# Delta rule: the inverse of the triangular systems kept as 64 columns per row

## The chip, the cores and the metric

The kernel runs on one core of a Trainium2 chip. The metric is the device time of one execution in microseconds, from launch to the last output. Three runs of the kernel before took 1076.86, 1078.5 and 1078.3 us; the median is 1078.3 us. The profiled execution is a further one, with its own time.

A core has a matrix engine (TensorE, PE in the rows), a vector engine (VectorE, DVE), a scalar engine (ScalarE, ACT), GpSimd (POOL) and SyncE (SP), which issues the transfers. Each works off its own queue in order and waits on semaphores for the others. TensorE takes its operands from the on-chip memory SBUF and writes to PSUM, eight banks of 128 partitions by 512 floats. Every matmul has a weight load ahead of it (rows named PEld), which can overlap the matmul before. A plain float32 product of this kernel is recorded as two loads and two matmuls, a product of rounded float32 halves and a transpose as one of each.

## The reference, cut to what matters

One layer of a hybrid encoder for 512 prompt rows and 64 sample rows: a gated delta rule (4 heads of 128) beside a differential attention, then attention to a memory, then a feed-forward block, with norms between. The change is in the delta rule. For each head it works on chunks of rows and solves two triangular systems:

```python
a_sys = jnp.where(strict, bc[..., :, None] * kk * gam, 0.0) + jnp.eye(C)
u = lax.linalg.triangular_solve(a_sys, bc[..., None] * vc, lower=True, unit_diagonal=True)
w = lax.linalg.triangular_solve(a_sys, (bc * jnp.exp(G))[..., None] * kc, lower=True, unit_diagonal=True)
```

after which a scan over the chunks carries the state: `vn = u - w S`, the output `qg S + qk vn`, and the new `S`.

## The kernel before, in words

The 576 rows (512 and 64) are worked through in five delta-rule chunks: four of 128 rows and the last of 64. The reference's chunk is 64 rows; a chunk of 128 is the same recurrence with a larger system. The order of the whole kernel: input norm and its transposes, projections of k, q and v with a short convolution, the gates, the norm of the memory rows, then `gdn_prep` and `gdn_scan` for the chunks, with the projection of z (`project_z`) and, later in the program, the projections and heads of the attention. After that come the output projection, the attention to the memory and the feed-forward block, all of them long rows of projections (`project`).

`gdn_prep` prepares one chunk: transposes of k, q and v, the decay matrix `gam`, the system `At` (transposed, strictly upper triangular, four heads side by side), and then its inverse by doubling (lines 595 to 643). The inverse is held twice: `X`, upper triangular, and `Dt`, its transpose. `masked(lv)` picks out of `At` the entries that couple two blocks of lv rows; `lev` holds the level of each entry. At the start `X` is the identity minus level 1, and `Dt` its transpose. Each level lv = 2, 4, 8, 16, 32 then does, for the four heads:

1. `by` = product of the masked `B` (weights) and `Dt` (moving), copied to `Y` by ScalarE (line 619);
2. `bx` = product of `X` (weights) and `Y` (moving), subtracted from `Dt` by VectorE (line 624);
3. four transposes of `Dt`, copied to `X` by ScalarE (line 628).

Level 64, the last doubling, only fills the block of `X` above the diagonal (lines 634 to 642). Until then both 64-row halves of a 128-row system are separate: `X` and `Dt` are block diagonal with two blocks of 64 by 64, and the other two quarters of each are zeros, which are multiplied and copied along. In the last chunk, of 64 rows, there is one block, and the level 32 is its last.

The products of a chunk go to one PSUM bank, `g0` for even chunks and `g1` for odd ones, each with one buffer. So a chunk's next product waits until the bank's last one is read. Two chunks' preparations run beside each other, one in each bank. The scans use the bank `gs`; the projections use `pr`, three buffers.

What sets the order: the framework's planner draws it at build time, from the order of the program, the dependencies and its own durations for the instructions; an instruction that is ready in that plan goes ahead of a later one. Around the change no order is written out by hand (that is only so in the opening, `in_order`). Semaphores are then placed for that fixed order on each engine. All matmuls carry line 99 and all transposes line 105, those of the helpers `mm` and `tr`.

Of the kernel before, what the change touches and what calls it, by code (L numbers as in the profile page):

```python
# [11 lines left out]
ALU = mybir.AluOpType  # L12
# [3 lines left out]
P = 128  # L16
# [8 lines left out]
H = 4  # L25
# [9 lines left out]
def hybrid_layer_kernel(  # L35
# [10 lines left out]
    V, A, G = nc.vector, nc.scalar, nc.gpsimd  # L46
# [28 lines left out]
    def nm(s):  # L75
        uid[0] += 1
        return f"{s}_{uid[0]}"
# [6 lines left out]
    def small(tag, shape, bufs=None):  # L84
        tag = SHARED.get(tag, tag)
        bufs = 1 if tag in ("vn", "on", "S") or tag[:-1] in ("At", "Dt", "Y") else 2
        return sp.tile(shape, F32, tag=tag, name=nm(tag), bufs=bufs)
# [4 lines left out]
    def bank(tag="ba"):  # L92
        return ps.tile([P, 512], F32, tag=tag, name=nm(tag), bufs=BANKS[tag])
# [4 lines left out]
    def mm(out, lhsT, rhs, start=True, stop=True, pin=False):  # L98
        i = nc.tensor.matmul(out, lhsT, rhs, start=start, stop=stop)  # L99
        if pin:  # L100
            tc.keep_in_program_order(i)

    def tr(out, in_, pin=False):
        n = in_.shape[0]
        i = nc.tensor.transpose(out, in_, ident[:n, :n])  # L105
        if pin:
            tc.keep_in_program_order(i)

    def bc(col, shape):
        return col.to_broadcast(shape)  # L110
# [110 lines left out]
    def turn(src, n, q, tag):  # L221

        b = bank(tag)
        for i in range(4):
            tr(b[:, i * P : i * P + n], src[:n, (4 * q + i) * P : (4 * q + i + 1) * P])
        return b.rearrange("p (i t) -> p i t", i=4)[:, :, :n]
# [138 lines left out]
    for typ in (1, 0, 2):  # L365
        cT[typ] = unit({1: 4, 0: 5, 2: 6}[typ], [P, 4, T])
        for h in range(H):
# [7 lines left out]
            n = SOFF + DEC  # L375
# [106 lines left out]
    for bi in range(2):  # L482
        scale(mn[:, bi, :], mt[:, bi, :], root(squares(mn[:, bi, :], mt[:, bi, :], P), P), gkv, P)
        for q in range(2):
            src = turn(mn[:, bi, :], P, q, "ba")
# [5 lines left out]
    with tc.issue_after(opened[mybir.EngineType.DVE]), tc.issue_after(opened[mybir.EngineType.Pool]):  # L491
        lev = const([P, P], "lev")
        prev = ident
        for lb in range(7):
            s = 2 << lb
            e = small("X", [P, P])
            G.memset(e, 1.0)
# [16 lines left out]
    def v4(ap, n):  # L514
        return ap.rearrange("p (h n) -> p h n", h=4)[:, :, :n]

    def sb(tag, bufs=2):
        return small(tag, [P, 4, P], bufs)
# [10 lines left out]
    def gdn_prep(c, c0, n):  # L529
        L = slice(c0, c0 + n)  # L530

        def st(tag):
            return sb(dict(gam="Y", sq="B", eg="B").get(tag, tag) + str(c % 2))

        r8 = tiny([P, 8], "tg")
        s8 = tiny([P, 8], "tg")
        bk = bank(f"g{c % 2}")
        for h in range(H):
            tr(bk[:n, h * P : (h + 1) * P], ck[:, h, L])
        kd = sb("kd")  # L540
        V.tensor_tensor(kd[:n], v4(bk, P)[:n], kdc[:n, c, :].unsqueeze(2).to_broadcast([n, 4, P]), ALU.mult)
        sq = st("sq")
        A.activation(sq[:n], v4(bk, P)[:n], AF.Square)
        V.tensor_reduce(s8[:n, 0:4], sq[:n], AX.X, ALU.add)
        bq = bank(f"g{c % 2}")
        for h in range(H):
            tr(bq[:n, h * P : (h + 1) * P], cq[:, h, L])
        sq2 = st("sq")
        A.activation(sq2[:n], v4(bq, P)[:n], AF.Square)
        V.tensor_reduce(s8[:n, 4:8], sq2[:n], AX.X, ALU.add)  # L550
        V.tensor_scalar(s8[:n], s8[:n], EPS, None, ALU.add)
        rpow(r8[:n], s8[:n])
        brk = tiny([P, 4], "tg")
        V.reciprocal(brk[:n], s8[:n, 0:4])
        V.tensor_tensor(brk[:n], brk[:n], beta[:n, c, :], ALU.mult)

        bg = bank(f"g{c % 2}")
        for h in range(H):
            mm(bg[:, h * P : h * P + n], bc(gg[:n, c, h : h + 1], [n, P]), triu[:n, :n])
        gam = st("gam")  # L560
        for h in range(H):
            V.tensor_scalar(
                gam[:n, h, :n], bg[:n, h * P : h * P + n], Gc[:n, c, h : h + 1], 0.0, ALU.subtract, ALU.min
            )
        A.activation(gam[:n, :, :n], gam[:n, :, :n], AF.Exp)
        G.tensor_tensor(gam[:n, :, :n], gam[:n, :, :n], triu[:n, :n].unsqueeze(1).to_broadcast([n, 4, n]), ALU.mult)
        bkk = bank(f"g{c % 2}")
        for h in range(H):
            mm(bkk[:n, h * P : h * P + n], ck[:, h, L], ck[:, h, L])
        At = st("At")  # L570
        for h in range(H):
            V.scalar_tensor_tensor(
                At[:n, h, :n], bkk[:n, h * P : h * P + n], brk[:n, h : h + 1], gam[:n, h, :n], ALU.mult, ALU.mult
            )
        bkq = bank(f"g{c % 2}")
        for h in range(H):
            mm(bkq[:n, h * P : h * P + n], ck[:, h, L], cq[:, h, L])
        KQ = sb("KQ")
        V.tensor_tensor(KQ[:n, :, :n], v4(bkq, n)[:n], gam[:n, :, :n], ALU.mult)
        nk, rq2 = tiny([P, 4], "tg"), tiny([P, 4], "tg")  # L580
        V.tensor_tensor(nk[:n], s8[:n, 0:4], r8[:n, 0:4], ALU.mult)
        V.tensor_scalar(r8[:n, 4:8], r8[:n, 4:8], P ** -0.5, None, ALU.mult)
        V.tensor_tensor(rq2[:n], r8[:n, 4:8], r8[:n, 4:8], ALU.mult)
        bv = bank(f"g{c % 2}")
        for h in range(H):
            tr(bv[:n, h * P : (h + 1) * P], cv_[:, h, L])
        vb = sb("vb")
        V.tensor_tensor(vb[:n], v4(bv, P)[:n], nk[:n].unsqueeze(2).to_broadcast([n, 4, P]), ALU.mult)
        if c > 0:
            eg = st("eg")  # L590
            A.activation(eg[:, :, :n], v4(bg, n), AF.Exp)
            G.tensor_tensor(ck[:, :, L], ck[:, :, L], eg[:, :, :n], ALU.mult)
            G.tensor_tensor(cq[:, :, L], cq[:, :, L], eg[:, :, :n], ALU.mult)  # L593

        def masked(lv):
            B = st("B")
            V.scalar_tensor_tensor(  # L597
                B[:n, :, :n], lev[:n, :n].unsqueeze(1).to_broadcast([n, 4, n]), float(lv), At[:n, :, :n],
                ALU.is_equal, ALU.mult,
            )  # L600
            return B

        X = sb("X")
        Dt = st("Dt")
        B = masked(1)
        V.tensor_tensor(X[:n, :, :n], ident[:n, :n].unsqueeze(1).to_broadcast([n, 4, n]), B[:n, :, :n], ALU.subtract)
        bt = bank(f"g{c % 2}")
        for h in range(H):
            tr(bt[:n, h * P : h * P + n], X[:n, h, :n])
        A.copy(Dt[:n, :, :n], v4(bt, n)[:n])  # L610
        lv = 2
        while lv < n:
            Y = st("Y")
            by = bank(f"g{c % 2}")
            if lv < 64:
                B = masked(lv)
                for h in range(H):
                    mm(by[:n, h * P : h * P + n], B[:n, h, :n], Dt[:n, h, :n])
                A.copy(Y[:n, :, :n], v4(by, n)[:n])
                bx = bank(f"g{c % 2}")  # L620
                if 2 * lv < n:
                    for h in range(H):
                        mm(bx[:n, h * P : h * P + n], X[:n, h, :n], Y[:n, h, :n])
                    V.tensor_tensor(Dt[:n, :, :n], Dt[:n, :, :n], v4(bx, n)[:n], ALU.subtract)  # L624
                    bt = bank(f"g{c % 2}")
                    for h in range(H):
                        tr(bt[:n, h * P : h * P + n], Dt[:n, h, :n])
                    A.copy(X[:n, :, :n], v4(bt, n)[:n])  # L628
                else:
                    for h in range(H):  # L630
                        mm(bx[:n, h * P : h * P + n], Y[:n, h, :n], X[:n, h, :n])
                    V.tensor_tensor(X[:n, :, :n], X[:n, :, :n], v4(bx, n)[:n], ALU.subtract)
            else:
                for h in range(H):
                    mm(by[64:, h * 64 : h * 64 + 64], At[:64, h, 64:], Dt[:64, h, :64])
                A.copy(Y[64:, :, :64], by[64:, :256].rearrange("p (h n) -> p h n", h=4))
                bx = bank(f"g{c % 2}")
                for h in range(H):
                    mm(bx[:64, h * 64 : h * 64 + 64], Y[64:, h, :64], X[64:, h, 64:])
                V.tensor_scalar(  # L640
                    X[:64, :, 64:], bx[:64, :256].rearrange("p (h n) -> p h n", h=4), -1.0, None, ALU.mult
                )
            lv *= 2
        return dict(kd=kd, vb=vb, X=X, KQ=KQ, brk=brk, rq=r8[:, 4:8], rq2=rq2)
# [291 lines left out]
    cols, rB = norm_columns(), const([P, T], "rB")  # L936
# [16 lines left out]
    for h in range(H):  # L953
# [8 lines left out]
        for t, (q0, _) in enumerate(QT):  # L962
            t0, n = TT[t]
# [7 lines left out]
            p = small("p0", [P, 512])  # L971
# [3 lines left out]
            bt = bank()  # L975
# [23 lines left out]
    cols, rB = norm_columns(), const([P, T], "rB")  # L999
# [90 lines left out]
    for m in range(KT):  # L1090
        last_block(m, pend, *HALVES[1])
        if m == 1:
            r = final_roots((0, 1), pin=True)
# [7 lines left out]
    r = final_roots((2, 3, 4))  # L1101
# [37 lines left out]
```

## Time and profile before

| | |
|---|---|
| median of three runs | 1078.3 us |
| profiled execution | 1076.9 us, its span from first to last instruction 1075.2 us |
| mean granted TensorE clock | 0.996 |
| matmul and weight-load instructions | 7504 each |
| weight reads and other reads from memory | 79.14 MB, 83 GB/s over the span with the writes |
| doubling products and transposes | first at 143.1 us, last at 284.8 us after the span's start |

A row of groups has the line, the engine, the operation, the tiles written and read, the shape, the count, then busy time in us and the mean duration of one in ns, then the engine's idle time just before them with what ended it. For TensorE the shape is weights (rows*columns), then the moving side. Matmuls overlap each other, so their durations are longer than the distance between them. A row of waits has the engine and tile, the instruction that released it, the total in us, the number of waits and the longest. A row of the timeline has the start in us, the length in us, the engine, the line, and a count where instructions of one kind follow each other.

### The profile page before, as it was taken

The page shows a single profiled execution, that of the slowest core. Times are in us where ns is not written, and L with a number is a line of the kernel's source. Part 1 is how long each engine was busy: PE and PEld are TensorE (multiplying, and loading weights), DVE is VectorE, ACT ScalarE, POOL GpSimd, SP SyncE. Part 2 cuts the span into 40 slices and gives each one's busy share as a digit, 9 for nine tenths or more (in the row PEclk, how much of TensorE's full clock was granted, in tenths as well). Part 3 has the DMA queues.
Part 4 walks back from the last instruction along what each step waited for, and adds up shares of the span by engine and source line. Part 5 has one row for each costly group of instructions (what it writes and reads, how often), then busy time and mean ns, then how long its engine had stood idle before and what let it go on. Part 6 is the DMA issues. An engine that isn't in the chain of part 4 may idle for free.

```text
span 1075.2 us, 18514 instructions
## 1 busy us (share of the span) xinstructions
PE 1043.5 (97%) x7504; PEld 982.4 (91%) x7504; DVE 625.2 (58%) x1347; ACT 401.3 (37%) x824; POOL 69.9 (6%) x126
## 2 busy tenths in 40 slices
PE   6999989899999999999999999999999999999996
PEld 5999989888888877999888899999999999999996
DVE  6756783666466765564554555555555555555654
ACT  5433644333246566443333443222222222222344
POOL 3311120222000000000000000000000000000000
PEclk9999999999999999999999999999999999999999
DMA  7242410010132265625111122132324141313312
GB/s 208 66 148 60 133 36 21 25 37 21 40 100 62 62 189 158 194 80 157 40 52 48 40 81 77 50 102 65 100 59 118 50 118 49 110 51 114 91 50 89
DMA packets 139448, 90.06 MB, mean 84 GB/s; under 512 B 5522, under 2 KB 130576, under 8 KB 138852
## 3 DMA queue, kind: packets, MB, share of 16 engines
q1 hardware_dynamic: 139364, 88.89, 28.3%
q8 instruction: 59, 0.97, 0.4%
q14 instruction: 25, 0.20, 0.1%
HBM read 79.14 MB, written 9.74 MB: 83 GB/s over the span
## 4 chain that ended last, share of the span: by engine, by line
PE 87%; issue 5%; DVE 3%; POOL 2%; DMA 1%; SPq 1%; ACT 1%; POOLq 0%; DVEq 0%; ACTq 0%
PE pr L99 69%; PE g L99 8%; PE gs L99 3%; PE ba L105 3%; PE ba L99 2%; PE g L105 2%; DMA raw<-in_w_in_dram 1%; POOL tg L185 1%; DVE B L597 1%; SPq L120 0%; POOL tiny L185 0%; DVE wl L153 0%; DVE u L213 0%; DVE Dt L624 0%; POOL u L593 0%
## 5 line engine op out<-in xcount | busy, mean ns | idle before, releaser
L99 PE MATMUL pr<-u,wh 128*128 128x256 f32 (+1 forms) x3552 | 733.1, 300 | 0.4 <-DVE u L269 0.3
L99 PEld LDWEIGHTS pr<-u,wh 128*128 128x128 f32 x3552 | 575.3, 190 | 5.8 <-issue 2.4
L99 PE MATMUL pr<-u,wl 128*128 128x256 f32 (+1 forms) x1776 | 529.3, 299 | 0.0
L99 PEld LDWEIGHTS pr<-u,wl 128*128 128x128 f32 x1776 | 336.0, 190 | 2.0 <-issue 0.7
L152 ACT CAST wh<-raw 128x1024 fp32r<-128x1024 f32 (+1 forms) x153 | 136.5, 892 | 269.6 <-PE pr L99 249.6
L153 DVE TENSOR_TENSOR wl<-raw,wh 128x1024 fp32r<-128x1024 f32 (+1 forms) x153 | 157.4, 1029 | 60.2 <-ACT wh L152 57.9
L901 DVE TENSOR_TENSOR u<-u,pr 128x256 f32<-128x256 f32 (+1 forms) x160 | 72.2, 453 | 102.1 <-PE pr L99 101.4
L1010 DVE TENSOR_TENSOR p<-pr,rB 128x256 f32<-128x256 f32 x64 | 29.3, 458 | 63.2 <-PE pr L99 63.2
L178 ACT CAST u<-p 128x256 fp32r<-128x256 f32 x64 | 27.8, 434 | 88.7 <-DVE p L1011 86.9
L185 POOL TENSOR_TENSOR tiny<-tiny,nhalf 128x1 f32<-128x1 f32 (+4 forms) x11 | 8.5, 773 | 670.1 <-DVE tiny L1069 413.3
L99 PE MATMUL pr<-wh,u 128*128 128x512 f32 x128 | 42.0, 404 | 0.0
L179 DVE TENSOR_TENSOR u<-p,u 128x256 fp32r<-128x256 f32 x64 | 29.3, 457 | 20.2 <-ACT u L178 20.2
L99 PE MATMUL pr<-u,u 128*128 128x256 f32 (+1 forms) x240 | 34.9, 305 | 0.0
L99 PEld LDWEIGHTS pr<-u,u 128*128 128x128 f32 x240 | 33.4, 197 | 0.0
L1011 DVE SCALAR_TENSOR_TENSOR p<-p 128x256 f32<-128x256 f32 x64 | 29.3, 458 | 1.7
L99 PE MATMUL g<-u,qz 128*128 128x256 f32 (+4 forms) x96 | 29.6, 411 | 0.3 <-ACT p L810 0.3
L628 ACT COPY X<-g 128x512 f32<-128x512 f32 (+1 forms) x24 | 13.2, 550 | 41.0 <-PE g L105 38.1
L379 DVE SCALAR_TENSOR_TENSOR p<-p,gcol,p 128x579 f32<-128x579 f32 x33 | 27.1, 822 | 1.1
L99 PEld LDWEIGHTS pr<-wh,u 128*128 128x128 f32 x128 | 23.4, 188 | 4.5 <-issue 0.2
L181 ACT ACTIVATE u<-u,gcol 128x256 fp32r<-128x256 f32 (+1 forms) x32 | 17.1, 534 | 23.5 <-DVE u L901 23.5
L99 PE MATMUL g<-Dt,B 128*128 128x128 f32 (+1 forms) x200 | 25.6, 272 | 0.1
L99 PE MATMUL pr<-wl,u 128*128 128x512 f32 x64 | 25.6, 400 | 0.0
(284 smaller groups left out, 1075.8 us busy)
## 6 DMA issues: line engine op xcount, KB each, us to landing
raw<-in_w_ff_dram SPq DMA_DIRECT2D x32, 512.0 KB
raw<-in_w_ff_dram SPq DMA_DIRECT2D x64, 256.0 KB
raw<-in_w_in_dram SPq DMA_DIRECT2D x28, 512.0 KB
raw<-in_w_mem_k_dram SPq DMA_DIRECT2D x8, 512.0 KB
raw<-in_w_mem_v_dram SPq DMA_DIRECT2D x8, 512.0 KB
raw<-in_w_out_dram SPq DMA_DIRECT2D x8, 512.0 KB
raw<-in_w_mem_q_dram SPq DMA_DIRECT2D x8, 512.0 KB
raw<-in_w_mem_o_dram SPq DMA_DIRECT2D x8, 512.0 KB
```

The source lines that it names most:

```text
L99: i = nc.tensor.matmul(out, lhsT, rhs, start=start, stop=stop)
L105: i = nc.tensor.transpose(out, in_, ident[:n, :n])
L152: A.copy(wh, raw)
L153: V.tensor_tensor(wl, raw, wh.bitcast(F32), ALU.subtract)
L178: A.copy(h, src)
L179: V.tensor_tensor(lo, src, h.bitcast(F32), ALU.subtract)
L181: A.activation(h, src, AF.Identity, scale=g)
L185: G.tensor_tensor(out, in_, bc(nhalf[: in_.shape[0], 0:1], list(in_.shape)), ALU.pow)
L379: V.scalar_tensor_tensor(yv[:, :n], cb[:, i : i + n], cwt[:, m, i : i + 1], yv[:, :n], ALU.mult, ALU.add)
L901: V.tensor_tensor(hm, hm, b, ALU.add)
L1010: V.tensor_tensor(f, b, rB[:, a0 : a0 + n], ALU.mult)
L1011: V.scalar_tensor_tensor(f, f, 0.0, f, ALU.max, ALU.mult)
```

## The change

For a chunk of 128 rows, `Dt` and `Y` are kept as 64 columns per row, those of the row's own diagonal block (`w` is 64, `cols` the columns 64 to 127). `X`, the weights of the second product, stays a full 128 by 128 matrix. Both products of the levels 2 to 32 thus have 64 moving columns in place of 128, and the same weights. Their four heads lie side by side in 256 columns of the bank (`tight`).

- `Y` is copied by ScalarE with 256 columns instead of 512.
- The subtraction on VectorE reads 64 columns per head from `Dt` and from the bank and writes each result twice, to columns 0 to 63 and 64 to 127 of `Dt`. A full 128 by 128 transpose of it then has the transposed blocks on its diagonal (and repeats of them beside it).
- The copy out of the transposes is split (`turn_blocks`): only the diagonal blocks are copied, the upper one (partitions 0 to 63) by ScalarE, the lower one (partitions 64 to 127) by VectorE, 64 partitions by 256 elements each. The zeros of `X` beside its blocks stay from its first writing. The first copy to `Dt` (line 610) is split in the same way.
- The last chunk has `w` = 64 = n: one block, one copy by ScalarE, sizes as before; its results lie 64 instead of 128 columns apart in the bank.

```diff
+        w = n // 2 if n == P else n
+        blocks = [slice(i, i + w) for i in range(0, n, w)]
+        cols = slice(n - w, n)
+
+        def tight(bank_):
+            return bank_[:n, : 4 * w].rearrange("p (h n) -> p h n", h=4)
+
+        def turn_blocks(dst, src, spread):
+            bt = bank(f"g{c % 2}")
+            for h in range(H):
+                tr(bt[:n, h * P : h * P + n], src[:n, h, :n])
+            for i, bl in enumerate(blocks):
+                to = dst[bl, :, bl if spread else cols]
+                (V.tensor_copy if i else A.copy)(to, v4(bt, n)[bl, :, bl])
...
-        bt = bank(f"g{c % 2}")
-        for h in range(H):
-            tr(bt[:n, h * P : h * P + n], X[:n, h, :n])
-        A.copy(Dt[:n, :, :n], v4(bt, n)[:n])
+        turn_blocks(Dt, X, False)
...
-                    mm(by[:n, h * P : h * P + n], B[:n, h, :n], Dt[:n, h, :n])
-                A.copy(Y[:n, :, :n], v4(by, n)[:n])
+                    mm(by[:n, h * w : h * w + w], B[:n, h, :n], Dt[:n, h, cols])
+                A.copy(Y[:n, :, cols], tight(by))
...
-                        mm(bx[:n, h * P : h * P + n], X[:n, h, :n], Y[:n, h, :n])
-                    V.tensor_tensor(Dt[:n, :, :n], Dt[:n, :, :n], v4(bx, n)[:n], ALU.subtract)
-                    bt = bank(f"g{c % 2}")
-                    for h in range(H):
-                        tr(bt[:n, h * P : h * P + n], Dt[:n, h, :n])
-                    A.copy(X[:n, :, :n], v4(bt, n)[:n])
+                        mm(bx[:n, h * w : h * w + w], X[:n, h, :n], Y[:n, h, cols])
+                    twice = [n, 4, n // w, w]
+                    V.tensor_tensor(
+                        Dt[:n, :, :n].rearrange("p h (r w) -> p h r w", w=w),
+                        Dt[:n, :, cols].unsqueeze(2).to_broadcast(twice),
+                        tight(bx).unsqueeze(2).to_broadcast(twice), ALU.subtract,
+                    )
+                    turn_blocks(X, Dt, True)
...
-                    mm(by[64:, h * 64 : h * 64 + 64], At[:64, h, 64:], Dt[:64, h, :64])
+                    mm(by[64:, h * 64 : h * 64 + 64], At[:64, h, 64:], Dt[:64, h, cols])
```

## Prediction

> **What bounds the kernel now.** I read the page's head and its table of busy time first, then the busy time of the engines in the stretch where the changed code runs (130 to 300 us), then that stretch's groups, its waits, and single bursts in the timeline.
>
> ```profile
> span 1075.2 us, 18514 instructions
> PE 1043.5 (97%) x7504; PEld 982.4 (91%) x7504; DVE 625.2 (58%) x1347; ACT 401.3 (37%) x824; POOL 69.9 (6%) x126
> ```
> ```profile
> core 0: us, PE busy (x) PEld busy (x) DVE busy (x) ACT busy (x) POOL busy (x), PEclk, DMA share, GB/s
> 130.00:300.00 170.00, 161.44 (x1297) 145.73 (x1297) 105.48 (x228) 63.08 (x110) 31.37 (x28) 1.00 0.13 38
> ```
>
> TensorE is busy nearly everywhere, and in the stretch of the change too: 161.44 of 170 us, at the full granted clock. It is idle there for 170 − 161.44 = 8.6 us. VectorE is at 105.48/170 = 62%, ScalarE at 37%. So the chain of a triangular system is long, but TensorE has projections to run beside it. A shorter chain buys time only where TensorE waits for the chain, or if the chain's own TensorE work shrinks.
>
> What the change touches, in the groups of the stretch by shape:
>
> ```profile
> L99 PE MATMUL g<-Y,X 128*128 128x128 f32 x160 | 22.6, 284 | 0.2
> L99 PE MATMUL g<-Dt,B 128*128 128x128 f32 x160 | 22.2, 284 | 0.1
> L99 PEld LDWEIGHTS g<-Y,X 128*128 128x128 f32 x160 | 19.5, 191 | 2.3 <-ACT Y L619 1.6
> L99 PEld LDWEIGHTS g<-Dt,B 128*128 128x128 f32 x160 | 19.4, 191 | 2.3 <-ACT X L628 1.6 <-ACT Dt L610 0.2
> L624 DVE TENSOR_TENSOR Dt<-Dt,g 128x512 f32<-128x512 f32 x20 | 13.7, 684 | 12.1 <-PE g L99 12.1
> L619 ACT COPY Y<-g 128x512 f32<-128x512 f32 x20 | 11.7, 587 | 14.7 <-PE g L99 12.7 <-issue 2.0
> L628 ACT COPY X<-g 128x512 f32<-128x512 f32 x20 | 11.7, 587 | 34.1 <-PE g L105 31.3 <-DVE tiny L923 2.8
> L610 ACT COPY Dt<-g 128x512 f32<-128x512 f32 x4 | 2.3, 587 | 8.6 <-PE g L105 8.6
> L628 ACT COPY X<-g 64x256 f32<-64x256 f32 x4 | 1.5, 366 | 6.9 <-PE g L105 6.8
> L751 DVE COPY u<-pr 128x256 f32<-128x256 f32 x2 | 0.8, 414 | 0.0
> L748 DVE COPY qz<-pr 64x256 f32<-64x256 f32 x2 | 0.8, 413 | 0.3 <-PE pr L99 0.3
> L748 ACT COPY qz<-pr 64x256 f32<-64x256 f32 x2 | 0.7, 368 | 2.4 <-DVE qz L748 2.4
> L99 PEld LDWEIGHTS g<-Dt,B 64*64 64x64 f32 x40 | 2.7, 134 | 0.8 <-ACT X L628 0.4 <-ACT Dt L610 0.2 <-issue 0.2
> L691 DVE SCALAR_TENSOR_TENSOR u<-gs,gcol,u 128x512 f32<-128x512 f32 x4 | 3.0, 750 | 3.5 <-PE gs L105 3.5
> ```
>
> And what TensorE waits for there before it can load weights:
>
> ```profile
> PEld g L105 <- DVE vb L588: 3.1, 2, 1.9
> PEld g L99 <- ACT X L628: 2.2, 10, 0.3
> PEld g L99 <- DVE At L572: 2.1, 1, 2.1
> PEld gs L99 <- DVE on L687: 2.0, 3, 1.1
> PEld g L99 <- ACT Y L619: 2.0, 8, 0.3
> PEld gs L99 <- DVE on L655: 1.4, 1, 1.4
> PEld ba L105 <- DVE u L213: 1.1, 1, 1.1
> PEld g L105 <- DVE Dt L624: 0.7, 2, 0.5
> ```
>
> **The products (320 instructions).** Chunks 0 to 3 run five levels with two products of four heads; a product is two instructions, which gives 4 × 5 × 2 × 4 × 2 = 320, the two x160 groups. Their moving side goes from 128 to 64 columns, their weights stay 128 by 128. Whether that is faster depends on what spaces the instructions. Four bursts of weight loads:
>
> ```profile
> 146.35 0.97 PEld L99 LDWEIGHTS g<-Dt,B 128*128 128x128 f32 x8
> 146.45 1.06 PE L99 MATMUL g<-Dt,B 128*128 128x128 f32 x8
> 279.20 0.54 PEld L99 LDWEIGHTS g<-Dt,B 64*64 64x64 f32 x8 [0.19 <-ACT X L628]
> 1066.20 0.52 PEld L99 LDWEIGHTS ba<-ones,p 128*128 128x128 f32 x4 [0.84 <-issue]
> 1066.23 0.58 PE L99 MATMUL ba<-ones,p 128*128 128x1 f32 x4 [0.60 <-DVE p L914]
> ```
>
> Columns are start, length, engine, line, count. The eight loads of today start (0.97 − 0.19)/7 = 0.111 us apart. At 1066 us the matmuls have a single moving column and weights of 128 columns, and the loads still start (0.52 − 0.19)/3 = 0.110 us apart. At 279 us the last chunk has 64 weight columns and 64 moving ones; a load takes about 0.134 us (its group's mean) and they start (0.54 − 0.134)/7 = 0.058 us apart. So the weights' columns set the pace here, not the moving ones, and 64 moving columns on 128-column weights should stay at 0.110 to 0.111. I take 0 for the 320 instructions. Bounds: 320 × (0.111 − 0.110) = 0.3 us gain from the nearer row, 320 × (0.111 − 0.058) = 17 us from the farther one.
>
> The Trainium skill, "TensorE: Matmul & The Clock Gate", section "LDWEIGHTS (loading the stationary operand)", charges a load by its weight columns over 1.2 GHz; that is an estimate of 107 ns for 128, whatever moves, and by it the sum gets 0. The same page's section "Back-to-back issue gap" charges the matmul by its moving columns, so by that section alone the bursts would about halve. The trace's row with one moving column agrees with the first; the second is the first rival below.
>
> **The copies on ScalarE.** Y goes from 128x512 to 128x256 and keeps ScalarE: 0.587 to about 0.37 us (0.368 is the 64x256 row; the width counts, as VectorE's 128x256 and 64x256 rows, 0.414 and 0.413, show), 20 times: 4.4 us of ScalarE, 0.22 us a step. X and Dt are split: ScalarE copies the upper block (0.366), VectorE the lower (0.413), 24 times. ScalarE itself is not the bound, so its 4.4 + 24 × 0.22 = 9.7 us are worth nothing in themselves; what counts are the waits. One level today:
>
> ```profile
> 219.02 0.58 ACT L628 COPY X<-g 128x512 f32<-128x512 f32 x1 [2.44 <-PE g L105]
> 219.65 0.97 PEld L99 LDWEIGHTS g<-Dt,B 128*128 128x128 f32 x8 [0.26 <-ACT X L628]
> 220.91 0.59 ACT L619 COPY Y<-g 128x512 f32<-128x512 f32 x1 [0.86 <-PE g L99]
> 221.54 0.97 PEld L99 LDWEIGHTS g<-Y,X 128*128 128x128 f32 x8 [0.22 <-ACT Y L619]
> 222.20 1.19 DVE L583 TENSOR_TENSOR tg<-tg 128x4 f32<-128x4 f32 x1
> 224.04 0.42 PEld L105 LDWEIGHTS g<-ident,Dt 128*128 128x128 f32 x4 [0.52 <-DVE Dt L624]
> ```
>
> Each burst starts as soon as its copy ends, and the loads stand still for 0.2 to 0.3 us before it; the rest of the copy is hidden by projections. For Y the group names 1.6 us of such waits in the changed shape; 0.22 us off each copy covers a wait of 0.2 to 0.3 us nearly whole. Y: −1.6 us (bounds 0, where the build's planner, which draws the order from its own durations, puts less cover behind a shorter copy; and −2.0).
>
> **X and Dt, split over two engines.** With VectorE free the step ends 0.587 − 0.413 = 0.17 us earlier. VectorE runs its queue in order and is busy 62% of the stretch; an instruction such as L624's (0.684) has on average half of it left, so the expected delay is 0.62 × 0.34 = 0.21 us and the step ends 0.04 us later: 0 on TensorE. Bounds: all 1.6 + 0.2 us of X and Dt waits gained; or one whole 0.684 us instruction always ahead, 0.684 + 0.413 − 0.587 = 0.51 us late, 24 times 12 us of chain, of which 10 of 24 steps show today that TensorE stands at that place: 5 us lost. Queued behind the lower-block copy is the next masked B or another chunk's work, and the result bank of that chunk's parity (one buffer) stays taken until both halves are read, so the next product waits for it too.
>
> **VectorE's load.** 24 × 0.413 = 9.9 us more, 105.5 to 115.4, up 9.4%. TensorE's waits on VectorE, the rows vb, At, on (two), u and Dt above, are 3.1 + 2.1 + 2.0 + 1.4 + 1.1 + 0.7 = 10.4 us; raised by the same share they cost 1.0 us. Bounds: 0, where the copies fall into VectorE's idle 64 us; 5 us, where half of them push a waited-for result. The subtraction of Dt (L624) still writes 128x512, from operands repeated by a zero step: 0 change; if it ran like L691's (0.750) it would cost 20 × 0.066 = 1.3 us of VectorE.
>
> **Moves.** No DMA moves, no SP or POOL instruction changes. The transposes keep their four instructions. The last chunk (64 rows) keeps its sizes, one block, one ScalarE copy.
>
> **Sum.** 0 (products) − 1.6 (Y) + 0 (X, Dt) + 1.0 (VectorE) = −0.6 us. The profiled execution took 1076.9 us (span 1075.2 and 1.7 around it): 1076.3 for such a one. The runs' median is 1078.3, 1.4 above it; carried over, the forecast is **1077.7 us**, no measurable change. Within 0.2% (2.2 us, about what a measurement here tells from none) counts as the same. Its own range, with X at +1.5 or −1 and the order redrawn a little: 1075.8 to 1080.
>
> **Rivals.**
> *The moving columns do set the pace.* Spacing 0.058 as in the 64x64 burst: −17 us, 1061. For it: that burst. Against: it has 64 weight columns, and the one-column burst kept 0.110. 5%.
>
> *The waits of the chain go.* With three shorter steps in each level and the order drawn anew, TensorE no longer stands behind Y, X and Dt: 2.0 + 2.2 + 0.7 = 4.9 us gained, nothing paid on VectorE, which has 64 idle us: 1073.4. For it: nearly all those waits are of 0.2 to 0.3 us, less than or near what the copies save. Against: 62% of VectorE. 30%.
>
> *VectorE's half ends the step late.* At the X and Dt steps, L628 and L610 of today, the lower block waits in VectorE's queue. It decides once more than 0.17 us stands ahead of it; with a whole instruction ahead it costs 5 us exposed as worked out, less 1.6 for Y: +3.4, 1081.7. For it: at 222.20 a VectorE instruction stood 1.19 us and TensorE then waited 0.52 for Dt. Against: ScalarE's waits show long gaps at this place (34.1 us before 20 copies), so the build's planner can often place the copy first. 24%.
>
> **How the numbers follow.** Forecast 41%, first rival 5%, second 30%, third 24%. Faster takes the first two rivals and little of the forecast's edge: 0.36; slower the third: 0.24; same 0.40. The range leaves out the first rival and the outer parts of the two others: 1072.6 to 1082.
>
> **What would show it.** Products: the groups with 128x64 matmuls on 128x128 weights, loads still 0.11 us apart (wrong if near 0.06). Y: copies at 0.37 us and its row of waits near 0. X and Dt: two groups, 0.37 and 0.41 us, and among TensorE's waits a row for the VectorE half: below 2 us as forecast, near 5 for the third rival. VectorE's busy time up by 10 us, ScalarE's down by 10. The forecast is wrong if TensorE's idle time in the stretch moves by more than 2 us, or if the order of projections outside it changes.

## Result and profile after

The changed kernel takes 1083.95 us (median of 4 runs, 1083.04 to 1086.03), the kernel before 1078.35 us (4 runs). The ratio is 1.0058, with a 95% interval of 1.0040 to 1.0075: slower by 0.6%, outside the predicted range. The profiled execution after took 1084.2 us.

The head and the table of busy time of the page after:

```profile
span 1082.4 us, 18534 instructions
PE 1044.9 (97%) x7504; PEld 982.2 (91%) x7504; DVE 639.2 (59%) x1371; ACT 391.8 (36%) x824; POOL 70.0 (6%) x126
```

The span grew by 7.2 us. TensorE's idle time in it went from 1075.2 − 1043.5 = 31.7 us to 1082.4 − 1044.9 = 37.5 us: 5.8 us of the 7.2 are idle time, and 1.4 us are the same 7504 matmuls taking longer. Where? The busy time of the engines by stretches, in the kernel after (columns as in the prediction: busy time and count of PE, PEld, DVE, ACT and POOL, granted clock, DMA share, GB/s):

```profile
130.00:300.00 170.00, 161.13 (x1327) 148.92 (x1325) 116.41 (x245) 54.27 (x110) 29.75 (x26) 1.00 0.15 43
300.00:350.00 50.00, 45.85 (x283) 38.17 (x282) 27.87 (x87) 21.66 (x65) 2.42 (x3) 0.93 0.22 66
350.00:450.00 100.00, 97.46 (x531) 77.61 (x530) 65.69 (x170) 59.92 (x168) 5.19 (x5) 1.00 0.43 141
320.00:325.00 5.00, 3.64 (x27) 3.10 (x26) 3.22 (x14) 1.72 (x5) 0.00 (x0) 1.00 0.27 99
325.00:330.00 5.00, 3.72 (x12) 2.27 (x11) 2.13 (x11) 2.37 (x12) 0.00 (x0) 0.60 0.01 2
330.00:335.00 5.00, 5.00 (x19) 3.47 (x18) 2.54 (x12) 2.31 (x10) 0.00 (x0) 0.72 0.00 0
```

and in the kernel before:

```profile
300.00:350.00 50.00, 49.71 (x333) 43.63 (x331) 30.75 (x105) 28.67 (x92) 1.27 (x2) 1.00 0.31 86
350.00:450.00 100.00, 98.91 (x564) 82.68 (x565) 62.58 (x150) 56.76 (x145) 4.53 (x5) 1.00 0.52 157
```

In the stretch of the change TensorE is idle 8.9 us, against 8.6: no loss shows there. The loss is behind it. Idle time from 300 to 350 us rises from 0.3 to 4.1 us, from 350 to 450 from 1.1 to 2.5 us, and from 326.0 to 332.8 us the granted clock is halved, which shows as 0.60 and 0.72 in the two stretches of 5 us. Laid beside each other by the number of weight loads done, the traces say the same: the changed kernel is 0.9 us ahead at load 2100 (290 us) and 2.6 us ahead at load 2300 (319 us), then 5.3 us behind at load 2400 (341 us), 7.4 at load 2700, and 7.3 at the end.

What stands at those places, first in the timeline of TensorE before (start, length, engine, line, instructions, and in brackets the idle time ahead with what ended it):

```profile
297.15 1.16 PE L99 MATMUL gs<-vn,kd 64*128 64x128 f32 x8 [0.87 <-DVE on L687]
...
307.87 1.52 PE L99 MATMUL g<-u,qz 128*128 128x256 f32 x8
```

then after:

```profile
307.86 1.16 PE L99 MATMUL gs<-vn,kd 64*128 64x128 f32 x8 [0.82 <-DVE on L703]
...
319.15 1.52 PE L99 MATMUL g<-u,qz 128*128 128x256 f32 x8
...
322.40 0.36 PE L99 MATMUL pr<-u,wl 128*128 128x256 f32 x1
323.56 0.55 PE L105 MATMUL ba<-ident,p 128*128 128x128 f32 x3 [0.80 <-DVE p L831]
324.67 0.71 PE L99 MATMUL gs<-u,aT 128*128 128x128 f32 x4 [0.57 <-ACT aT L838]
325.22 0.39 PE L99 MATMUL gs<-vs,aT 128*128 128x128 f32 x2
326.58 2.08 PE L99 MATMUL g<-u,qz 128*128 128x256 f32 x4 [0.97 <-ACT p L826]
...
331.16 0.88 PE L99 MATMUL pr<-u,wh 128*128 128x320 f32 x2
```

`gs<-vn,kd` is the last product of the delta rule's scan, `g<-u,qz` the first of the attention heads, which use the delta rule's banks `g0`, `g1` and `gs` and come behind it. Both stand 11 us later. Then, between 322.4 and 331.2 us, no projection (`pr`) starts: the attention is alone on TensorE, which waits for its softmax steps (`p`, `aT`).

And what TensorE had done instead: the projections since 120 us, up to that first attention product, as the trace groups them by tile, before and after (the two halves of the weights, count, durations in ns, first and last start):

```profile
L99 PE MATMUL pr<-u,wh x280: 276/308/416, 119.9 to 307.6; 128*128 128x320 f32 x70, 128*128 128x256 f32 x70
L99 PE MATMUL pr<-u,wl x140: 278/308/415, 119.7 to 307.3; 128*128 128x320 f32 x71, 128*128 128x256 f32 x69
```
```profile
L99 PE MATMUL pr<-u,wh x340: 276/308/417, 119.7 to 318.8; 128*128 128x320 f32 x86, 128*128 128x256 f32 x84
L99 PE MATMUL pr<-u,wl x170: 278/307/415, 121.7 to 318.9; 128*128 128x320 f32 x86, 128*128 128x256 f32 x84
```

510 instead of 420 (two of each count began just before 120 us). Such matmuls start 0.147 us (320 columns) or 0.118 us (256) apart, as three start every 0.44 or 0.355 us in a run of them; at a mean of 0.132 us, 90 more take 11.9 us, which is the delay of 11.3 us. So the delta rule did not become slower work on TensorE. The plan put 90 more projections ahead of the first attention product, and they were missing later.

The changed code itself, in the groups of the stretch 130 to 310 us after:

```profile
L99 PEld LDWEIGHTS g<-Y,X 128*128 128x128 f32 x160 | 19.7, 191 | 2.3 <-ACT Y L633 1.1
L99 PEld LDWEIGHTS g<-Dt,B 128*128 128x128 f32 x160 | 19.5, 191 | 2.8 <-DVE X L618 2.2 <-DVE Dt L618 0.2
L639 DVE TENSOR_TENSOR Dt<-Dt,g 128x512 f32<-128x512 f32 x20 | 13.7, 687 | 11.0 <-PE g L99 11.0
L618 ACT COPY X<-g 64x256 f32<-64x256 f32 x24 | 8.8, 365 | 41.5 <-PE g L105 41.3
L618 DVE COPY X<-g 64x256 f32<-64x256 f32 x20 | 8.6, 428 | 4.1 <-ACT X L618 3.5
L633 ACT COPY Y<-g 128x256 f32<-128x256 f32 x20 | 7.5, 373 | 28.5 <-PE g L99 27.3 <-issue 1.1
```

The loads of the products take 19.5 and 19.7 us (19.4 and 19.5 before). In the row of VectorE's copy the idle time ends with ScalarE's copy of the other block: the two halves don't run at the same time. One such step in the timeline after:

```profile
173.49 0.36 ACT L618 COPY X<-g 64x256 f32<-64x256 f32 x1 [2.35 <-PE g L105]
...
173.89 0.43 DVE L618 COPY X<-g 64x256 f32<-64x256 f32 x1 [0.69 <-ACT X L618]
...
174.37 0.97 PEld L99 LDWEIGHTS g<-Dt,B 128*128 128x128 f32 x8 [0.21 <-DVE X L618]
```

From 173.49 to 174.32 us the step takes 0.83 us, where the single copy took 0.587. In the trace all 24 of VectorE's copies wait on ScalarE's semaphore, so this holds for each step. TensorE's waits before it loads weights, from 130 to 300 us after:

```profile
PEld g L105 <- DVE vb L588: 2.4, 2, 1.8
PEld g L99 <- DVE X L618: 2.2, 4, 0.8
PEld g L99 <- DVE At L572: 2.1, 1, 2.1
PEld gs L99 <- DVE on L703: 2.0, 2, 1.0
PEld g L99 <- ACT Y L633: 1.5, 7, 0.3
PEld ba L105 <- DVE u L213: 1.1, 1, 1.1
...
PEld g L105 <- DVE Dt L639: 0.7, 1, 0.7
...
PEld g L99 <- ACT X L618: 0.2, 1, 0.2
```

### The profile page after: what moved, and what is told of

It is laid out like the page before. It is cut to its first block, busy times and chain, and to the rows that moved or that the text cites. A ratio compares the mean times of both kernels' runs of the same rounds, so it can differ in the third digit from the quotient of the medians.

```text
span 1082.4 us, 18534 instructions
## 1 busy us (share of the span) xinstructions
PE 1044.9 (97%) x7504; PEld 982.2 (91%) x7504; DVE 639.2 (59%) x1371; ACT 391.8 (36%) x824; POOL 70.0 (6%) x126
## 4 chain that ended last, share of the span: by engine, by line
PE 83%; DVE 6%; issue 5%; POOL 2%; ACT 1%; DMA 1%; POOLq 0%; DVEq 0%; SPq 0%; ACTq 0%
PE pr L99 66%; PE g L99 8%; PE ba L105 3%; PE gs L99 2%; PE ba L99 2%; PE g L105 2%; DVE wl L153 1%; POOL tg L185 1%; DMA u<-in_cache_mem_k_dram 1%; DVE p L379 1%; POOL tiny L185 0%; DMA u<-in_x_prompt_dram 0%; DVE u L269 0%; DVE B L597 0%; ACT wh L152 0%
## 5 line engine op out<-in xcount | busy, mean ns | idle before, releaser
L99 PE MATMUL pr<-wh,u 128*128 128x512 f32 x128 | 44.5, 414 | 0.5 <-ACT u L893 0.5
L99 PE MATMUL g<-u,qz 128*128 128x256 f32 (+4 forms) x96 | 32.1, 439 | 1.2 <-ACT p L826 1.2
L826 ACT ACTIVATE p<-g,ta 128x320 f32<-128x320 f32 (+4 forms) x40 | 21.0, 529 | 14.2 <-DVE ta L824 11.6
L99 PE MATMUL g<-Dt,B 128*128 128x64 f32 (+1 forms) x200 | 24.6, 265 | 1.3 <-DVE X L618 1.2
L99 PEld LDWEIGHTS g<-Dt,B 128*128 128x128 f32 (+1 forms) x200 | 22.1, 180 | 3.7 <-DVE X L618 2.2
```

Of the source, the lines that this page charges most:

```text
L826: A.activation(p[:, :nk], b[:, :nk], AF.Exp, bias=mx[:, c : c + 1], scale=0.125, accum_out=l[:, c : c + 1])
```

## Experiments

The theories at the start: A, the two halves of the split copy take turns at one bank, each level gets longer by 0.25 us, and the delta rule ends later; B, VectorE's load holds the chain up; C, the plan's order changed because the products have fewer moving columns, and the projections lie elsewhere. The runs at the end test what became of C. The two columns after the ratio give the starts of the last copy to `X` and of the first attention product. The last column counts the recorded projection matmuls that start from 120 us to the first attention product; a ratio is to runs of the kernel before in the same series; "idle" is TensorE's, from 300 to 350 us.

| kernel | median us | ratio to before [95%] | last copy of the solve, us | first attention product, us | idle, us | projections by then |
|---|---|---|---|---|---|---|
| before | 1078.2 | | 282.6 | 307.9 | 0.3 | 418 |
| after | 1084.0 | 1.0058 [1.0040, 1.0075] | 295.6 | 319.2 | 4.1 | 508 |
| both blocks by ScalarE | 1083.1 | 1.0042 [1.0027, 1.0057] | 291.4 | 317.9 | 4.5 | 500 |
| split copy alone | 1080.1 | 1.0016 [1.0006, 1.0026] | 290.7 | 317.3 | 1.9 | 474 |
| after, X in one copy | 1079.7 | 1.0016 [1.0007, 1.0026] | 287.4 | 315.4 | 3.9 | 477 |
| two banks | 1102.0 (one run) | | 306.8 | 335.3 | 7.2 | 531 |
| after, 128 moving columns | 1078.2 | 0.9999 [0.9989, 1.0009] | 290.2 | 315.0 | 0.9 | 449 |
| the same, X in one copy | 1079.0 | 1.0009 [0.9999, 1.0018] | 285.9 | 313.5 | 0.9 | 445 |
| 64 moving columns alone | 1077.5 | 0.9999 [0.9989, 1.0010] | 286.4 | 312.0 | 2.8 | 478 |
| after, v held | 1097.1 | 1.0174 [1.0157, 1.0191] | 299.0 | 326.8 | 6.5 | 399 |
| after, k and v held | 1112.2 | 1.0314 [1.0299, 1.0330] | 307.0 | 334.0 | 8.5 | 344 |
| before, v held | 1080.6 | 1.0024 [1.0014, 1.0033] | 283.5 | 308.9 | 0.6 | 396 |
| 128 moving columns, v held | 1086.7 | 1.0082 [1.0067, 1.0097] | 290.3 | 316.4 | 4.8 | 402 |
| after, third buffer of q | 1084.6 | 1.0060 [1.0039, 1.0081] | 296.6 | 319.9 | 1.5 | 517 |
| after, moved rows alone | 1086.7 | 1.0073 [1.0054, 1.0092] | 297.2 | 320.8 | 4.2 | 519 |
| before, third buffer of q | 1076.8 | 0.9982 [0.9973, 0.9992] | 283.3 | 308.6 | 0.0 | 420 |

### Both blocks copied by ScalarE

```diff
-                (V.tensor_copy if i else A.copy)(to, v4(bt, n)[bl, :, bl])
+                A.copy(to, v4(bt, n)[bl, :, bl])
```

> The changed kernel, with both blocks of each copy out of the transposes on ScalarE. Theory A (the two readers of one bank take turns: a split step is 0.365 + 0.43 us and a hand-over, about 0.85, against 0.587 in one copy; the delta rule ends late and TensorE runs out of projections beside the first attention head): a step of 0.365 + 0.365, about 0.73 to 0.79, between the two, so the last products of the delta rule come between those of before (297 us) and of the changed kernel (308 us), and the time is 1079 to 1083. Theory B (VectorE's 10 us more are to blame): all of it gone, 1077 or less.

1083.1 us, ratio 1.0042. VectorE's copies are gone, and its busy time from 130 to 300 us is 104.7 us, below the 105.5 of before; most of the loss remains. So neither VectorE's load nor the place in its queue (B) makes the loss.

### The split copy alone, in the kernel before

```diff
-                    A.copy(X[:n, :, :n], v4(bt, n)[:n])
+                    for i, bl in enumerate(blocks):
+                        (V.tensor_copy if i else A.copy)(X[bl, :, bl], v4(bt, n)[bl, :, bl])
```

> The kernel before, all matrices at 128 columns, with only the copy of X split over ScalarE (upper block) and VectorE (lower block). Theory A: the longer step alone, without the shorter copies of Y: the delta rule ends as late as in the changed kernel or 2 to 4 us later, 1083 to 1087. Theory B: nearly all of the 10 us of VectorE are here too, 1082 to 1084. Theory C (the products or copies of 64 columns are to blame): 1077 to 1079, as before.

1080.1 us, ratio 1.0016. The waits of VectorE's copy in this kernel, from 130 to 320 us:

```profile
DVE X L632 <- ACT X L632: 5.1, 11, 1.2
```

The halves take turns here too, more often than after (3.5 us in 8 waits), but the kernel loses only 1.7 us. The turn-taking alone (A) doesn't explain 5.6 us.

### The change with X in one copy

```diff
+            if spread:
+                A.copy(dst[:n, :, :n], v4(bt, n)[:n])
+                return
```

> The changed kernel, with X copied from the transposes in one ScalarE copy of 128x512. The quarters of X beside the blocks then hold repeats in place of zeros, so the inverse is not the delta rule's; the instructions and sizes are otherwise those of the changed kernel. Theory A: the X step is back at 0.587 and Y's copy is 0.37, so the delta rule ends earlier than before (290 to 297 us) and the time is 1073 to 1078. Theory B: VectorE is loaded with only the four copies to Dt, 1076 to 1078. Theory C: 1083.

1079.7 us, ratio 1.0016, between what A and C had forecast. Without the split of X three quarters of the loss go, though the products still have 64 columns. Read with the run before it: either half of the change costs little alone. The idle time from 300 to 350 us is not the whole account: it is 3.9 us here, nearly as after, but TensorE is idle only 5.2 us from 130 to 300 us, where it was 8.9 after.

### Two banks for the two blocks

```diff
-            bt = bank(f"g{c % 2}")
-            for h in range(H):
-                tr(bt[:n, h * P : h * P + n], src[:n, h, :n])
+            bts = [bank(f"g{c % 2}" if i == 0 else "ba") for i in range(len(blocks))]
+            for i, (bt, bl) in enumerate(zip(bts, blocks)):
+                for h in range(H):
+                    if i:
+                        mm(bt[bl, h * P : h * P + w], src[bl, h, bl], ident[bl, bl])
+                    else:
+                        tr(bt[bl, h * P : h * P + w], src[bl, h, bl])
...
-                (V.tensor_copy if i else A.copy)(to, v4(bt, n)[bl, :, bl])
+                (V.tensor_copy if i else A.copy)(to, v4(bt, w)[bl])
```

> The changed kernel, with the lower blocks turned into a second PSUM bank (those of the tag ba), by products of 64x64 with the identity, and the upper blocks by transposes of 64x64 into the bank of the chunk. If two readers of one bank take turns by the order that the build puts on a bank: VectorE's copies of the lower block no longer start behind ScalarE's of the upper one, and its row of waits on ScalarE (3.5 us, 8 waits in the changed kernel) goes. If it is X, the tile that both write, they still take turns. The time is no test here, since the turning costs TensorE 12 instructions in place of 4.

The lower block goes to the bank `ba`, with a product by the identity; a turn has 12 TensorE instructions instead of 4, so the time of 1102.0 us says nothing of the change. VectorE's copy in this kernel, from 130 to 320 us:

```profile
DVE X L622 <- PE ba L99: 15.3, 18, 1.4
```

It waits for its own bank's products: all 24 of VectorE's copies wait on TensorE's semaphore here and none on ScalarE's, though both engines still write one tile `X`. So the turns are taken at the shared bank, not at the tile. (The halves still don't run at the same time here, since the products of `ba` come behind the transposes.)

The Trainium skill, "PSUM — Partial Sum Buffer", section "PSUM bank collisions raise a hardware error", lets two engines access one bank at the same time if they are in different quadrants of 32 partitions. The two blocks lie in different ones and the traces of the change show the wait all the same, since the built program has it; no run here shows what the chip would do without.

### The change with 128 moving columns

```diff
+        def twofold(ap):
+            return ap.unsqueeze(1).to_broadcast([n, n // w, w])
...
-                    mm(by[:n, h * w : h * w + w], B[:n, h, :n], Dt[:n, h, cols])
+                    mm(by[:n, h * P : h * P + n], B[:n, h, :n], twofold(Dt[:n, h, cols]))
```

and the second product in the same way: the 64 columns are moved twice, by a zero step. The copies stay as in the change, and read the first 64 of each head's 128 result columns.

> The changed kernel, with each product's 64 moving columns read twice (a zero step), so that 128 move and only the first 64 of each result are used; copies and matrices as changed. Theory P (the build's planner charges a product by its moving columns, puts more projections between the products' steps, and the chip, which spaces them by the weight loads at 0.11 us, is then late with the delta rule and has no projections left beside the first attention head): the built order on TensorE has 352 projection matmuls from the first product of the solve to the first attention product, against 326 before and 417 in the changed kernel, so most of the loss goes: 1077 to 1080, no half-clock window near 326 us. Theory A (the turn-taking of the split copies, still here in full): 1082 to 1084.

1078.2 us, ratio 0.9999: the whole loss is gone, with the split kept. VectorE's copy in this kernel:

```profile
DVE X L621 <- ACT X L621: 7.0, 12, 1.4
```

Its waits are twice those of the change (3.5 us), and cost nothing. What differs is the order: 449 projections by the first attention product in place of 508, which starts at 315.0 in place of 319.2 us. More columns per product, as long on the chip, give a shorter kernel. This is what A and B can't say and C does.

### The same with X in one copy

The edits of the two kernels together.

> As the run with one copy of 128x512 to X (the quarters beside the blocks hold repeats, so the inverse is not the delta rule's), and with 128 moving columns by repeat. Theory P: 349 projection matmuls up to the first attention product (386 without the repeat); the X step is back at 0.587 and Y at 0.37, the delta rule ends no later than before, 1076 to 1078.5. Theory A: the same as without the repeat, 1079.7, since no copy differs.

1079.0 us, ratio 1.0009, not told apart from before or from 128 moving columns with the split.

### 64 moving columns alone, in the kernel before

```diff
-                    mm(by[:n, h * P : h * P + n], B[:n, h, :n], Dt[:n, h, :n])
-                A.copy(Y[:n, :, :n], v4(by, n)[:n])
+                    mm(by[:n, h * w : h * w + w], B[:n, h, :n], Dt[:n, h, :w])
+                A.copy(two(Y[:n, :, :n]), twice(by))
```

and so on, every copy and the subtraction with 512 columns as before.

> The kernel before, with only the moving side of the products cut to 64 columns: the left 64 columns of Dt and Y move, and the copies to Y and the subtraction from Dt read each result twice and stay 128x512, X one copy. The lower blocks are therefore not those of the delta rule. Theory P: the built order has 386 projection matmuls up to the first attention product against 326; the delta rule ends 5 to 10 us later and the time is 1079.5 to 1082. Theory A (no split copy here): 1077 to 1079. If the chip did gain from 64 moving columns: 1065 to 1075.

1077.5 us, ratio 0.9999. No loss, though the order moves as in the change: in its trace 290 projection matmuls stand between the first and the last product of the solve, against 222 before (326 after, 252 with 128 columns and the split). The forecast of C for this run, 1079.5 to 1082, missed. So C alone isn't the loss either: there is slack, and 478 projections by the first attention product, at 312.0 us, are within it.

### Projections held back

```diff
+    scan_end = [i for i in nc.cur_bb.bb.instructions if i.engine == mybir.EngineType.PE][-1]
...
-            project(weights(w2, base + h * P), xs, evac)
+            with tc.issue_after(scan_end) if h == 1 and kind in "v" else nullcontext():
+                project(weights(w2, base + h * P), xs, evac)
```

By then the theory was: the projections that cover other work are a stock, the change uses it up ahead, and with some of it kept back the hole at 322 us (the 8.8 us without a projection) closes. The projection of v of the second head (k and v in the second kernel) is held until the scan's last instruction on TensorE. The third and fourth kernel have the hold of v in the kernel before and in the one with 128 moving columns.

> The changed kernel, with the projection of v of the second attention head held back in TensorE's queue until the last instruction of the delta rule's scan (48 matmuls; the rest is unchanged). The built order then has 301 projection matmuls up to the first attention product, against 417 in the changed kernel and 326 before. Cover theory (the loss is what happens when the first attention head finds no projections left: idle TensorE, then half its clock): no half-clock window near 326 us, idle of TensorE from 300 to 350 us below 2 us (4.1 in the changed kernel), 1077 to 1080. If the later end of the delta rule by itself costs the time: 1082 to 1085.

> The same, with the projections of k and of v of the second head held back (96 matmuls; 253 in the built order up to the first attention product). Cover theory: the gain beside the first head is kept, but the delta rule now has less beside it, so TensorE's idle from 130 to 300 us rises above the 8.8 of the changed kernel: 1077 to 1082. If the later end by itself costs the time: 1082 to 1085.

> The kernel before, with the projection of v of the second head held back in the same way (301 in the built order, 326 without). Cover theory: it had cover enough at the first head (idle 0.3 us from 300 to 350 us), so nothing is gained there: 1077 to 1080.

> The changed kernel with 128 moving columns by repeat and the projection of v of the second head held back (301 in the built order, 352 without). Cover theory: 0.9 us of idle were left from 300 to 350 us, so at most 1 us is gained: 1077 to 1079.

All four got slower, the changed kernel most: 1.0174 and 1.0314. The first of them, while it ran out of projections:

```profile
284.00:322.00 38.00, 28.30 (x146) 21.41 (x146) 11.35 (x28) 5.65 (x13) 1.78 (x2) 0.51 0.10 26
```

No projection runs for 48.2 us from 271.1 us on; the end of the solve and the scan are alone, TensorE is idle for 9.7 of 38 us, and the clock is halved for 37.5 us from 284.5 us. The theory in that form, which had forecast 1077 to 1080 for this run, fell: the projections that the plan put into the solve's end and the scan are not too many there, they are needed there as much as later. To hold them moves the hole ahead and makes it larger. In the kernel before, whose delta rule ends 13 us earlier, the same hold costs 0.24%.

### A third buffer for q

```diff
-    qz = [cp.tile([P, 2, T], F32, tag=f"qz{i}", name=f"qz{i}") for i in range(2)]
+    qz = [cp.tile([P, 2, T], F32, tag=f"qz{i}", name=f"qz{i}") for i in range(3)]
...
-                        (A.copy if c else V.tensor_copy)(qz[h % 2][R, c, ts_], b[R])
+                        (A.copy if c else V.tensor_copy)(qz[h % 3][R, c, ts_], b[R])
```

The pause at 322 us comes where the third head's q waits for a buffer that the first head still reads. A third buffer takes that wait away; to make room, the sample rows of v move into the tails of two other tiles. The control has the moved rows alone.

> The changed kernel, with a third buffer qz for the queries of the attention heads (the place for it comes from keeping the sample's v rows in the unused ends of two other tiles). The projections of the third head can then run before the first head is done. Stock theory (the delta rule and the first head draw on one stock of projections, which ends at the third head's because the second buffer of qz is still read; the changed kernel has used it up at 322 us, 520 matmuls from 120 us on): the pause of projections of 8.8 us at 322 us goes, no half-clock window there, 1077 to 1080.5. If the later end of the delta rule costs by itself: 1082 to 1085.

> The changed kernel, with only the sample's v rows kept in those ends, and two buffers qz as before: the control of the run with a third buffer. Both theories: 1082 to 1085.

> The kernel before, with the third buffer qz. Stock theory: it did not run out (idle 0.3 us from 300 to 350 us), so little is gained: 1076.5 to 1078.5.

In the changed kernel the pause at 322 us is gone, but not the loss: 1.0060. Its stretches:

```profile
325.00:330.00 5.00, 5.00 (x35) 4.47 (x34) 1.63 (x4) 2.77 (x9) 0.00 (x0) 1.00 0.01 3
...
400.00:450.00 50.00, 45.27 (x209) 35.36 (x210) 30.22 (x64) 28.64 (x66) 2.60 (x2) 0.93 0.46 142
```

TensorE is busy throughout 325 to 330 us. From 395.6 us on no projection runs for 10.6 us, and the clock is halved for 6.8 us from 403.5 us. So the hole has moved and not closed; that the projections at hand end there is read from the trace and was not tested. The stock theory had forecast 1077 to 1080.5 for this run and missed; 1084.6 lies in the range given for the other case, that the later end of the delta rule costs by itself. The control shows the hole at 324.0 us, as the change. In the kernel before, the third buffer gives 0.9982 [0.9973, 0.9992], 0.2% below the kernel before and the lowest median of all kernels run here.

## Why the prediction was wrong

**The products: right.** Loads of 19.5 and 19.7 us with 64 moving columns are the 0 that was taken, and the first rival (−17 us) is out.

**The Y copy: right in kind.** The copy takes 0.373 us instead of 0.587, as forecast, but TensorE's waits for it went from 2.0 us in 8 waits to 1.5 us in 7, a gain of 0.5 and not 1.6. The prediction let 0.22 us off a copy cover a wait nearly whole; one wait is on average 0.21 us still. The lower bound's reason, less cover behind a shorter copy, would fit, and no run tests it.

**X and Dt: wrong, little by itself.** The step assumed that both halves run at the same time, and asked only when VectorE is free. They take turns: 0.83 us in place of 0.587. The row of the two copies to `qz`, with ScalarE's idle time ended by VectorE's copy of the same bank, stood among the lines quoted in the prediction and shows it; it was read for its duration only. TensorE's wait for the VectorE half, 2.2 us, still lies nearer the 2 of the forecast than the 5 of the third rival. X and Dt together went from 2.4 to 2.6 us (the rows of X, and 0.2 for Dt in the groups).

**VectorE's load: right that it is small, wrong in sign.** ScalarE's busy time fell by 9.5 us, as forecast; VectorE's rose by 14.0 (10 forecast), of which the 24 copies are 10.3. TensorE's waits on `vb`, `At`, `on`, `u` and `Dt` went from 10.4 to 8.3 us, where +1.0 was taken.

**Moves: the step that failed.** It says "No DMA moves", and of the order the prediction says only that it is "redrawn a little", within the forecast's own range. The sum of −0.6 us was for the stretch of the change, and there it held: +0.3 us of idle time. But the order that was redrawn around it put 90 more projections, 11.9 us of TensorE's time, ahead of the first attention product. In the prediction a projection beside the solve was cover at no price. It has one: what covers the solve is not there to cover the attention, and it lets the attention start 11.3 us later. Which of the two costs the time stays open (below). It showed in the sign that the last line of "What would show it" names: the order of projections outside the stretch changed.

**The third rival** gave 1081.7 us, nearest to the result, and is wrong as a mechanism: with no half on VectorE the ratio is still 1.0042.

**What the runs show of the cause.** Two parts of the change together, neither alone: the split copy alone +0.16%, 64 moving columns alone 0, both +0.58%. With the split kept and 128 columns moved, the loss is gone. The products' loads take 19.5 us a group there as before, so the order is what differs, and it carries the loss. In all kernels without a hold and with four transposes to a turn, the time follows the number of projections that are used by the first attention product: up to 478 the ratio lies between 0.9982 and 1.0016, at 500 to 519 between 1.0042 and 1.0073. Why the plan does so is read from the orders and not shown: a longer level leaves room for more projections beside it, and so do products with fewer columns, if the plan takes them for shorter. In the changed kernel's trace TensorE then idles at softmax steps of the attention, and the clock is halved for 6.8 us. The page's sums agree: 5.8 us of idle time, 1.4 us of slower matmuls.

**What stays open.** That the planner prices a matmul by its moving columns is inferred from the orders: 64 columns in place of 128 put 290 projections inside the solve in place of 222, and 326 in place of 252 with the split. Its prices weren't read. Between 478 and 500 the loss sets in, but whether it is the count, which projections they are, or the later start of the attention isn't told apart. The start sorts the same kernels as well: up to 317.3 us they lose at most 0.16%, from 317.9 us on at least 0.42%. And for the change the two are the same quantity, 11.3 us of delay and 11.9 us of projections. The runs meant to part them, the holds and the third buffer in the changed kernel, went against the stock theory's forecasts. Each kernel is one draw of the plan, and how far two plans differ by chance wasn't measured.

## What to carry to other kernels

Where TensorE is filled by a planner, a change of shapes is also a change of the plan: ask not only what an instruction costs on the chip, but what the plan puts around it, and which later stage that work was to cover. Look for the stage behind the change whose cover is finite (here the attention heads), and count what is left for it. In these builds two engines that copy from one PSUM bank take turns (0.83 us for the two halves, 0.587 for the whole), so a split copy is as long as both halves; a row with one engine's idle time ended by another engine's copy of the same bank is the sign of it.

## What the runs showed of the hardware

**The clock falls with idle time in small pieces.** After 322.4 us the recorded gaps of TensorE were 0.80, 0.57 and 0.97 us, none longer, and the clock was halved from 326.0 to 332.8 us. In the 3.4 us before 326.0 us the rows above leave TensorE idle for about 1.8 us. In other runs it was halved for 3.4, 6.8, 13.7 and up to 41.0 us, in multiples of about 3.4 us; the three longest (27.3, 37.5 and 41.0 us) in the runs with projections held back. The Trainium skill, "TensorE: Matmul & The Clock Gate", section "Part 1: The HAM clock gate (the "warmup" mystery)", has the clock halved after an idle window of about 3.4 us. The trace agrees on the half clock and on the length of a window; but here no recorded gap was that long, and a window with TensorE idle for about half of the time was enough.

**A shorter moving side is no shorter product, and a longer one no longer.** With weights of 128 columns and 64 moving ones, the eight loads at 174.37 us start (0.97 − 0.19)/7 = 0.111 us apart, as with 128 moving columns before. The groups' loads take 19.5 and 19.7 us after, and 19.5 and 19.5 us where the 64 columns are moved twice.
